# A hybrid decoder layer on one core: three steps of window attention instead of four and a half after each chunk of the input projection's last block

## The chip, the core and the metric

The kernel runs on one core of a Trainium2 chip. The metric is the device time of one execution in microseconds (us), the median of several runs. TensorE is called PE in the profile (PEld is its weight loads), VectorE is DVE, ScalarE is ACT, GpSimd is POOL, and SP issues the DMAs of this kernel.

## What is computed

One decoder layer over 2048 tokens of width 1024, in float32. Cut to what matters here:

```python
proj = rms_norm(x) @ w_in                     # 2176 columns = 17 chunks of 128
qa, ka, va, pb, qm = split_cols(proj, ...)
out_a = sliding_window_attention(qa, ka, va)  # 6 heads, blocks of 128 queries, 256 keys in the band
out_b = rwkv7_mixer(pb)                       # a recurrence over the tokens, 6 heads
out_m = memory_attention(qm, mk, mv)          # 4 heads, 256 memory tokens
x = x + concat(out_a, out_b, out_m) @ w_out
x = x + conv_ffn(rms_norm(x))                 # silu(gate) * val, then w_down
```

## The kernel before, in words

The tokens are cut into 4 blocks of 512 for the large products and into 16 tiles of 128 for attention and the recurrence (RWKV). Every large product takes three matmuls for one (each operand is split into a high and a low part: `whi`, `wlo`, `hh`, `hl`), so a chunk of the projection or of the output product is 24 matmuls of 128x512 (`proj`, which writes the PSUM tile `mm`).

**Input projection** (`ip`): for each block, 17 chunks in the order of `ORDER`; `g` counts the chunks from 0 to 67, so the last block is g = 51 to 67. After each chunk `post` reads the result out of PSUM. The last five chunks of each block (0, 1, 2, 15, 16) are the queries of the window and memory attention; they are split in `qhi` and `qlo`, stored to DRAM (`dq`), and the last of them starts a power on POOL that gives the queries' norms (`rsb`). In the last block all chunks go to one PSUM buffer, `mm`; in the others two take turns:

```python
o = self.proj(ps, w.pop(g), hh, hl, "mm" if g % 2 or b == NB - 1 else "po")
```

**Attention** (`attention`) is a generator with six steps for each of the 16 tiles of queries: window of the first kv head, window of the second, memory logits, values (two steps), and the rest of the memory attention. Tile i reads the queries of its own tokens, so tiles 12 to 15 need the last block of the projection, with its `dq` and `rsb`; tiles 0 to 11 do not. On PE it is `pl`, `tpa`, `po`, `plm`, `tpm` and `pm`; on DVE mostly `lg` and `em`.

**RWKV** (`rwkv`) is a second generator, four steps for a tile: front (`pz`, `pc`), `pg` and `tpb`, a triangular inverse of 31 times two small DVE operations (`xtmp`, `xinv`) between two trips through DRAM (`nbd` to `nb`, `xbd` to `xa`), and the chain over two half tiles (`pq`, `pu`, `pS`).

**Output product** (`outproj`): for each block of 512 it loads the concatenated results (`cr`), splits them (`ch`, `cl`) and runs 8 chunks with the weights `w_op`. Its pool of SBUF takes the place of the projection's pools, so it can begin to load only when the last chunk's `post` has let go of them. Block 0 of it needs tiles 0 to 3 of attention and RWKV, block 1 tiles 4 to 7, and so on. The feed-forward part follows.

**What sets the order.** All of this is recorded first, and a list scheduler (`Recorder.order`) then puts the instructions of each engine in order by dependencies and priorities. The order of recording counts in two ways: it decides who gets which buffer of a ring after whom (`slots`; the PSUM rings `ip` and `po` are shared by `post` and attention), and with that the length of the paths from which the priorities come. `side(g)` is called after chunk g and decides how many steps of RWKV and attention are recorded there; what is left of both is recorded after the projection, one step of each in turn, in `run`. Every instruction is issued through one helper, so all rows of the profile carry line 349, and the names of the tiles tell them apart.

Of the kernel before, what the change touches and what calls it, by code (L numbers as in the profile page):

```python
# [129 lines left out]
class Recorder:  # L130
# [93 lines left out]
    def margin(self, d, o):  # L224

        return 0 if d.eng == o.eng or None in (d.eng, o.eng) else MARGIN

# [33 lines left out]
    def run(self):  # L261
# [35 lines left out]
        while True:  # L297
# [17 lines left out]
            if soon[e] and o.dur > 150:  # L315
                c = min((c for c in soon[e] if c[0] < t + min(WAIT, o.dur) and c[2].level > o.level), default=None)
                if c:
# [41 lines left out]


WAIT = 100
MARGIN = 300
SLACK = 1500
WR = 4
# [49 lines left out]
class K:  # L414
# [1064 lines left out]
    def run(self):  # L1479
# [64 lines left out]
        atn = []  # L1544

        def side(g):
            for _ in range(starts.get(g, 0)):
                next(rw, None)
            if atn and (g - 52) * 72 // 16 >= 0:
                for _ in range((g - 51) * 72 // 16 - (g - 52) * 72 // 16):  # L1550
                    next(atn[0], None)
        for n, b in (("t", 2), ("w", 4), ("h", 1), ("x", 4)):
            p[n] = pool(n, b, side="right")
# [2 lines left out]
        def x_done():  # L1556
# [3 lines left out]
            p["a"] = pool("a", 2)  # L1560
            atn.append(self.attention(p, ps))
        self.ip(p, ps, side, x_done)
        for n in ("h", "w", "t"):
            rec.close(p[n])
# [130 lines left out]
```

## Time and profile before

| | |
|---|---|
| median of 3 runs | 2493.63 us (2492.27 to 2495.86) |
| profiled execution, its own time | 2499.48 us |
| its span, first to last instruction | 2497.6 us |
| mean granted TensorE clock | 0.968 of full speed |
| busy: PE, DVE, ACT, POOL | 95%, 81%, 49%, 8% of the span |

The span is what the rows further down lie in; the profiled execution's own time is 1.9 us longer, and 5.85 us above the median. Busy PE time is not PE at its peak, since matmuls overlap and are slower when the clock is lowered. Times in rows are us from the span's start.

### The profile page before, as it was taken

What the parts mean: (1) busy time and instruction counts of PE and PEld (TensorE: products, weight loads), DVE (VectorE), ACT (ScalarE), POOL (GpSimd) and SP (SyncE); (2) the same over time, 40 slices, a digit from 0 to 9 for tenths busy, and PEclk for the clock granted to TensorE, in tenths of its full rate; (3) what the DMA queues carried; (4) which work ended last, traced back from release to release, by engine and by line L of the source; (5) the groups of instructions that cost most, each with busy time, mean ns of one, the idle gap of its engine ahead of it and who ended that gap; (6) DMA issues with size and microseconds to landing.
All of it is one profiled execution on the core that took longest, in us unless ns stands there. A gap on an engine that the chain in (4) does not pass through costs nothing.

```text
span 2497.6 us, 36689 instructions
## 1 busy us (share of the span) xinstructions
PE 2372.4 (95%) x12268; PEld 1886.0 (76%) x12268; DVE 2015.2 (81%) x4614; ACT 1219.6 (49%) x2413; POOL 190.2 (8%) x292
## 2 busy tenths in 40 slices
PE   8899989899899979999899999999999998999999
PEld 6677777676666757777788888888888876888887
DVE  7579677878878777759588998899888887888876
ACT  6354544555445544555355455565555463444442
POOL 1112212211111121100000000000000000000000
PEclk9999999899989989999999999999999998999999
DMA  7586746744434465557233733354323246558443
GB/s 226 176 246 179 214 127 176 190 131 137 138 106 132 118 192 157 168 162 238 81 117 110 261 119 117 115 179 137 106 93 113 100 150 214 162 155 275 148 141 129
DMA packets 292933, 389.30 MB, mean 156 GB/s; under 512 B 49911, under 2 KB 155392, under 8 KB 292744
## 3 DMA queue, kind: packets, MB, share of 16 engines
q1 hardware_dynamic: 292744, 386.96, 49.8%
q8 instruction: 97, 1.59, 0.3%
q14 instruction: 92, 0.75, 0.1%
HBM read 274.89 MB, written 111.97 MB: 155 GB/s over the span
## 4 chain that ended last, share of the span: by engine, by line
PE 80%; DVE 8%; DMA 7%; issue 3%; ACT 1%; SPq 0%; POOL 0%; POOLq 0%; DVEq 0%; ACTq 0%
PE uf L349 28%; PE mm L349 16%; PE uch L349 14%; PE uip L349 7%; PE pq L349 4%; PE po L349 2%; PE pg L349 1%; DMA nb<-nbd 1%; PE tpa L349 1%; DVE xtmp L349 1%; DVE wlo L349 1%; PE pl L349 1%; PE st L349 1%; DVE xinv L349 1%; DMA wraw<-w_down_in 1%
## 5 line engine op out<-in xcount | busy, mean ns | idle before, releaser
L349 ACT CAST whi<-wraw 128x512 fp32r<-128x512 f32 (+1 forms) x410 | 250.2, 613 | 423.7 <-PE uf L349 148.9
L349 PE MATMUL uf<-h2h,wlo 128*128 128x512 f32 x1056 | 412.2, 392 | 15.3 <-DVE wlo L349 15.3
L349 PE MATMUL uf<-h2h,whi 128*128 128x512 f32 x1056 | 412.7, 392 | 4.7 <-ACT whi L349 4.6
L349 PE MATMUL uf<-h2l,whi 128*128 128x512 f32 x1056 | 412.6, 391 | 0.0
L349 DVE TENSOR_TENSOR wlo<-wraw,whi 128x512 fp32r<-128x512 f32 (+1 forms) x410 | 276.2, 677 | 89.1 <-ACT whi L349 87.7
L349 ACT CAST whi<-ws 128x512 fp32r<-128x512 f32 (+1 forms) x272 | 164.6, 609 | 288.5 <-PE uf L349 151.1
L349 DVE SCALAR_TENSOR_TENSOR uc<-ub,pp,uc 128x1024 f32<-128x1024 f32 x176 | 224.2, 1278 | 26.0 <-ACT uc L349 26.0
L349 PEld LDWEIGHTS uf<-h2h,wlo 128*128 128x128 f32 x1056 | 199.5, 189 | 59.0 <-DVE wlo L349 17.5
L349 PE MATMUL mm<-hh,whi 128*128 128x512 f32 x544 | 228.0, 420 | 15.6 <-DVE sh L349 5.4
L349 PEld LDWEIGHTS uf<-h2h,whi 128*128 128x128 f32 x1056 | 199.3, 189 | 48.4 <-ACT whi L349 6.4
L349 PEld LDWEIGHTS uf<-h2l,whi 128*128 128x128 f32 x1056 | 199.5, 189 | 41.8 <-DVE h2l L349 0.4
L349 PE MATMUL mm<-hl,whi 128*128 128x512 f32 x544 | 223.3, 411 | 2.0 <-DVE hl L349 1.9
L349 PE MATMUL mm<-hh,wlo 128*128 128x512 f32 x544 | 222.9, 410 | 0.0
L349 PE MATMUL uch<-h2h,whi 128*128 128x512 f32 x528 | 205.6, 389 | 0.0
L349 PE MATMUL uch<-h2h,wlo 128*128 128x512 f32 x528 | 205.5, 390 | 0.0
L349 PE MATMUL uch<-h2l,whi 128*128 128x512 f32 x528 | 205.4, 389 | 0.0
L349 DVE TENSOR_TENSOR wlo<-ws,whi 128x512 fp32r<-128x512 f32 (+1 forms) x272 | 178.5, 667 | 10.6 <-ACT whi L349 10.1
L349 PEld LDWEIGHTS mm<-hh,whi 128*128 128x128 f32 x544 | 106.6, 196 | 46.8 <-DVE sh L349 6.0
L349 ACT CAST h2h<-tr 128x512 fp32r<-128x512 f32 x182 | 110.0, 619 | 60.3 <-DMA tr<-dg 44.8
L349 ACT ACTIVATE uc<-ub,pp 128x1024 f32<-128x1024 f32 x88 | 109.4, 1244 | 38.4 <-DVE ub L349 37.1
L349 PEld LDWEIGHTS mm<-hl,whi 128*128 128x128 f32 x544 | 106.6, 196 | 25.8 <-DVE hl L349 3.4
L349 DVE TENSOR_TENSOR h2l<-tr,h2h 128x512 fp32r<-128x512 f32 x182 | 119.9, 684 | 7.3 <-ACT h2h L349 7.2
(363 smaller groups left out, 4702.8 us busy)
## 6 DMA issues: line engine op xcount, KB each, us to landing
wraw<-w_up_in SPq DMA_DIRECT2D x176, 256.0 KB
tr<-dg SPq DMA_DIRECT2D x154, 256.0 KB
wraw<-w_ip_in SPq DMA_DIRECT2D x136, 256.0 KB
dg<-uc SPq DMA_DIRECT2D x88, 256.0 KB
dg<-tt SPq DMA_DIRECT2D x66, 256.0 KB
wraw<-w_op_in SPq DMA_DIRECT2D x64, 256.0 KB
wraw<-w_down_in SPq DMA_DIRECT2D x64, 256.0 KB
xk<-xT_in SPq DMA_DIRECT2D x56, 256.0 KB
```

The costliest lines, as they stand in the source:

```text
L349: getattr(getattr(nc, o.eng), o.fn)(*map(real, o.a), **{k: real(v) for k, v in o.k.items()})
```

## The change

It changes how many attention steps `side` records after each of the 16 chunks g = 52 to 67: 72 steps over 16 chunks (4 or 5 after each, 12 tiles of attention in all) become 48 (3 after each, 8 tiles). The other 48 of the 96 steps, 24 more than before, are recorded after the projection with the rest of RWKV.

```diff
+EARLY = 48
...
-            if atn and (g - 52) * 72 // 16 >= 0:
-                for _ in range((g - 51) * 72 // 16 - (g - 52) * 72 // 16):
+            if atn and g >= 52:
+                for _ in range((g - 51) * EARLY // 16 - (g - 52) * EARLY // 16):
                     next(atn[0], None)
```

No instruction is added or removed: PE has 10764 matmuls, DVE 4614, ACT 2235 and SP 1594 instructions in both programs. On PE the first 667 and the last 6111 stand in the same order; the 3986 between them do not, because the priorities change. Counted in the order: the first matmul of the projection's last block with a recorded attention step (g = 52) is number 2071 before and 2250 now, its last number 3826 before and 3522 now, and the first of the output product number 3908 before and 3693 now.

The last matmuls on PE ahead of the output product's first, `mm<-ch`, in the program before. `pl` is the window logits of attention tile 12, the others belong to tile 11 and, `pz`, to RWKV:

```order
L349 MATMUL tpb<-cst,bk 128x128 x6
L349 MATMUL plm<-km,dq 128x256 x4
L349 MATMUL po<-pt,va 64x384 x2
L349 MATMUL pz<-w_488,lw 128x384
L349 MATMUL tpm_10276<-cst,em 128x128 x4
L349 MATMUL st<-cst,sq 128x128 x4
L349 MATMUL pm<-ptm,vm 64x128 x4
L349 MATMUL tpm_10329<-cst,em 128x128 x4
L349 MATMUL pm<-ptm,vm 64x128 x4
L349 MATMUL pl<-ka,dq 128x256 x10
L349 MATMUL mm<-ch,whi 128x512
```

The same place now; `tpa`, `po` and `plm` are of attention tile 8, and `pq`, `pc`, `pu` and `pS` are the RWKV chain and front:

```order
L349 MATMUL pS<-uv,bkt 64x64 x6
L349 MATMUL tpa<-cst,lg 128x128
L349 MATMUL pq<-uv,gmk 64x64 x5
L349 MATMUL po<-pt,va 64x384
L349 MATMUL pq<-S_112,ar 128x128 x3
L349 MATMUL tpa<-cst,lg 128x128 x5
L349 MATMUL pc<-cst,sg 128x130 x3
L349 MATMUL pu<-qa,X_124 64x64 x6
L349 MATMUL plm<-km,dq 128x256 x4
L349 MATMUL mm<-ch,whi 128x512
```

Between the last projection matmul and the first output matmul there stood 81 matmuls, and 170 stand there now, with more of attention (18 `tpa` instead of 12, 12 `plm` instead of 4) and of the RWKV chain (30 `pq` instead of 6, 18 `pu` instead of none). Attention tile 12, which needs the projection's last chunk, has moved behind. The 24 matmuls of the first output chunk are spread over 79 places instead of 30. Between the last matmul of one projection chunk and the first of the next, for the 15 boundaries from g = 52 to 67, stood 31 other matmuls on average and 10 at least; now it is 27 and 7.

The SP queue at the same place, before. `dq<-dq` is the load of attention tile 12's queries, `dq__1446<-qlo` the store of the last chunk's queries, `cr` the first loads of the output product:

```order
L349 DMA dq__1446<-qhi 64x4x128 x2
L349 DMA rr<-drk__714 128x1536
L349 DMA nbd_10243<-gmk 32x12x32 x2
L349 DMA dq__1446<-qlo 64x4x128 x2
L349 DMA va<-dv__1313 128x128
L349 DMA dcat__3560<-cat 128x384
L349 DMA dq<-dq__1446 128x2x640
L349 DMA cr<-dcat__3560 128x4x128 x3
L349 DMA nb<-nbd_10243 96x1x1024
L349 DMA xbd_10388<-xinv 96x256
L349 DMA wraw<-w_op_in 128x512
```

And now, where `dq<-dq` is the load of tile 8's queries:

```order
L349 DMA dq<-dq__1446 128x2x640
L349 DMA va<-dv__1313 128x128
L349 DMA nbd_9415<-gmk 32x12x32 x2
L349 DMA dq__1446<-qlo 64x4x128
L349 DMA dcat__3126<-cat 128x384
L349 DMA xa<-xbd_9171 32x6x32
L349 DMA uv<-dv__1313 64x384
L349 DMA cr<-dcat__3126 128x4x128 x2
L349 DMA nb<-nbd_9415 96x1x1024
L349 DMA dcat__3126<-cat 128x256
L349 DMA cr<-dcat__3126 128x4x128
L349 DMA wraw<-w_op_in 128x512
```

The load of the queries that the next attention tile reads has moved ahead of the last store `dq__1446<-qlo`, and the first loads of the output product keep their place behind that store.

## Rows read from the trace of the kernel before

**Rows 1.** Busy time by stage: stretch, its length, busy of each engine, PEclk, DMA.

```profile
146.00:464.00 318.00, 303.00 (x1818) 241.58 (x1817) 253.32 (x739) 153.63 (x321) 62.75 (x79) 0.98 0.61 181
464.00:864.00 400.00, 364.91 (x2515) 263.92 (x2515) 317.05 (x1224) 206.25 (x600) 69.34 (x125) 0.92 0.48 134
864.00:892.00 28.00, 17.65 (x119) 12.13 (x119) 23.69 (x105) 13.41 (x35) 8.64 (x3) 0.81 0.69 185
892.00:920.00 28.00, 22.72 (x98) 15.62 (x98) 22.08 (x81) 13.99 (x40) 3.97 (x12) 0.76 0.75 207
920.00:1061.00 141.00, 137.47 (x936) 102.88 (x936) 101.80 (x348) 69.51 (x178) 20.70 (x42) 0.98 0.54 161
```

**Rows 2.** The timeline around the projection's end: start, length, engine, operation, [idle before].

```profile
863.69 0.39 PE L349 MATMUL mm<-hh,wlo 128*128 128x512 f32 x1
...
873.83 1.25 SPq L349 DMA_DIRECT2D dq__1446<-qlo  x2
...
877.36 1.56 SPq L349 DMA_DIRECT2D cr<-dcat__3560  x3
...
879.50 6.85 POOL L349 TENSOR_TENSOR rsb<-rsb,mh 128x40 f32<-128x40 f32 x1 [1.72 <-DVE rsb L349]
...
882.63 0.62 ACT L349 CAST ch<-cr 128x512 fp32r<-128x512 f32 x1 [1.83 <-DMA cr<-dcat__3560]
...
886.39 0.88 DVE L349 SCALAR_TENSOR_TENSOR lg<-pl,rsb,bias 128x256 f32<-128x256 f32 x2 [0.74 <-POOL rsb L349]
...
889.60 0.19 DVE L349 TENSOR_TENSOR xtmp<-xinv,nb 96x31 f32<-96x31 f32 x1 [1.36 <-DMA nb<-nbd]
...
891.62 0.80 PE L349 MATMUL mm<-ch,whi 128*128 128x512 f32 x1 [2.53 <-ACT whi L349]
```

**Rows 3.** What PE waited for from 864 to 924: total, times, longest.

```profile
PE pl L349 <- DVE lg L349: 3.9, 1, 3.9
PE mm L349 <- ACT ch L349: 2.7, 1, 2.7
PE mm L349 <- ACT whi L349: 2.5, 1, 2.5
```

**Rows 4.** PE busy and clock in slices of 10 us.

```profile
870.00:880.00 10.00, 7.73 (x59) 1.00 0.67 184
880.00:890.00 10.00, 3.54 (x17) 0.57 0.95 250
910.00:920.00 10.00, 9.17 (x52) 0.66 0.29 100
```

**Rows 5.** PE's timeline: two neighbours at the lower clock, two at the full one.

```profile
681.68 0.63 PE L349 MATMUL mm<-hl,whi 128*128 128x512 f32 x1
682.11 0.63 PE L349 MATMUL mm<-hh,wlo 128*128 128x512 f32 x1
...
684.57 0.39 PE L349 MATMUL mm<-hl,whi 128*128 128x512 f32 x1
684.79 0.39 PE L349 MATMUL mm<-hh,wlo 128*128 128x512 f32 x1
```

**Rows 6.** Groups of PE instructions, 100 to 1210 us: busy, mean ns.

```profile
L349 PE MATMUL po<-pt,va 128*64 128x384 f32 x124 | 51.5, 528 | 1.7 <-DMA nbd<-gmk 0.9 <-ACT pt L349 0.7
L349 PE MATMUL tpa<-cst,lg 128*128 128x128 f32 x186 | 37.9, 308 | 6.4 <-DVE lg L349 5.7 <-ACT em L349 0.4
L349 PE MATMUL pl<-ka,dq 128*128 128x256 f32 x180 | 41.6, 324 | 9.6 <-DVE lg L349 8.0 <-DVE xtmp L349 1.5
L349 PE MATMUL pm<-ptm,vm 128*64 128x128 f32 x256 | 27.5, 292 | 1.9 <-ACT ptm L349 1.4 <-ACT cat L349 0.6
L349 PE MATMUL plm<-km,dq 128*128 128x256 f32 x128 | 25.4, 314 | 2.9 <-DVE lg L349 1.9 <-ACT pt L349 1.0
L349 PE MATMUL tpm<-cst,em 128*128 128x128 f32 x128 | 22.3, 290 | 2.8 <-DVE em L349 2.1 <-DVE xtmp L349 0.7
```

**Rows 7.** Reading a chunk out of PSUM, 464 to 864 us: groups of ACT and DVE.

```profile
L349 ACT ACTIVATE raw<-mm,om 128x512 f32<-128x512 f32 x10 | 6.8, 683 | 6.0 <-PE mm L349 6.0
L349 DVE SCALAR_TENSOR_TENSOR sh<-mm,pp,raw 128x511 f32<-128x511 f32 x6 | 4.5, 742 | 0.4 <-ACT carry L349 0.4
```

**Rows 8.** PE's waits from 480 to 800 us: the chunks of the projection on PSUM's readers.

```profile
PE mm L349 <- DVE sh L349: 4.1, 1, 4.1
```

## The prediction

> **What bounds the kernel now.** I read the page first, then the busy time by stage, then the timeline and PE's waits at the one stage that stands out, and last the order of the two programs. The page says that PE is the engine that sets the time (95% busy, 80% of the chain that ended last). The order says where the change can act: the first 667 and the last 6111 matmuls keep their places. In the trace that frozen part ends at about 146 us and begins again at about 1061 us, and every instruction is still there once. So only the 915 us between can change, and only through two things: how long PE idles there and at what clock it runs.
>
> The stages [rows 1] tell where that is. In the projection's last block (464 to 864 us) PE idles 400 - 364.9 = 35.1 us, 8.8%, at a mean clock of 0.92. From 864 to 892 it idles 10.3 of 28 us at 0.81, from 892 to 920 5.3 of 28 us at 0.76. After that, to 1061, 3.5 of 141 us (2.5%) at 0.98. The 56 us from 864 to 920 hold 15.6 of the 69.3 us of idle time in the whole stretch.
>
> Why there: twelve tiles of attention are recorded before the projection ends, and these are all that can run without its last block. The timeline [rows 2] shows all three sources of PE work dry at once. The last projection matmul is at 863.7; its queries are stored at 873.8, and only then come the output product's loads (877.4), their split (882.6) and its first matmul (891.6). Attention tile 12 waits for the queries' norms, 6.85 us on POOL from 879.5, so that its first `lg` is at 886.4. RWKV's next inverse waits for `nb` until 889.6. PE's longest waits [rows 3] are these: `pl` on `lg` 3.9 us, `mm` on `ch` 2.7 and on `whi` 2.5. The clock follows [rows 4]: 1.00 in the slice from 870, 0.57 in the next, in which PE was busy 3.5 of 10 us, and still 0.66 from 910, where PE was busy again.
>
> **The change part by part.** It costs nothing in instructions; four tiles of attention (8 to 11) are recorded after the projection instead of inside its last block. A tile is about 206/16 = 12.9 us of busy PE (the six groups of [rows 6] add to 206), so some 52 us of PE work move. The order also moves RWKV: 179 matmuls more now stand before chunk 52 (PE number 2250 instead of 2071), some two tiles of RWKV, and one tile more stands behind the projection.
>
> *The gap at the end of the projection.* Before, 81 matmuls stood in it, and PE was busy 17.65 us in those 28 us [rows 1], 0.218 us each. Now 170 stand there, so about 37 us of PE work, more than the 28 us that the stores, loads and splits take. Tile 8's queries and norms come from an earlier block, so it waits for neither `dq` nor `rsb`. I let this stretch keep the last block's own share of idling, 8.8%: 37 x 0.088 = 3.3 instead of 10.3, a gain of 7.0 us. From 892 to 920 the first output chunk now has 55 other matmuls among its 24 (it spans 79 places, before 30), so its waits for `ch` and `whi` are covered too: 28 x 0.088 = 2.5 instead of 5.3, a gain of 2.8. Then the clock. At the lower level, 1.2 GHz, a matmul takes 0.43 us, at 2.4 GHz 0.22 to 0.23 [rows 5], so a shortfall of the mean clock costs about its own share of the busy time. The stage lost 0.19 x 17.65 + 0.24 x 22.7 = 8.8 us; at the last block's 0.92 it would lose 0.08 x 51 = 4.1, a gain of 4.7. Together **-14.5 us**. The bounds are 0 (the new work waits as the old did) and -24.4 (15.6 + 8.8, no idling and full clock).
>
> *The stages around it.* The last block loses 304 matmuls (3826 - 3522, at 364.9/1756 = 0.208 us each 63 us busy, 69 us long): its idling falls by 69 x 0.088 = 6.1 us and its clock loss by 0.08 x 63 = 5.0. The stage before it gains 179 matmuls, 37 us, at its own rates (15 of 318 us idle, 0.98): +1.8 and +0.8. The stage after 920 grows from 141 to about 185 us (63 us moved behind, 19 of them in the gap) and has more attention and less dense work in it. Before, it idled 2.5%; the last block, with more attention, 8.8%. With the mean of the two, and of the clocks (0.95), it idles 10.5 us instead of 3.5 (+7.0) and loses 9.3 us of clock instead of 2.8 (+6.5). Sum -6.1 - 5.0 + 2.6 + 13.5 = **+5.0 us**. If it keeps its old rates, that is 4.6 and 3.7 us instead of 3.5 and 2.8, and the sum -6.5. If it takes the last block's rates (16.3 and 14.8), it is +16.3. I take the middle, since per us its new mix lies between the two stages.
>
> *The chunk boundaries.* All chunks of the last block use one PSUM buffer, so between two of them PE needs other work until ACT and DVE have read the first: 0.68 + 0.74 = 1.43 us [rows 7] when neither queues. Fewer attention steps could lay this bare. In the order they do not: between the chunks of g = 52 to 67 stand 31 other matmuls on average before and 27 now, at least 10 before and 7 now, and at 0.208 us seven are 1.46 us. The trace shows one real wait of this kind, 4.1 us [rows 8]. I price it at 0, since RWKV fills the places that attention left; with the cover gone at every one of the 15 boundaries it is 15 x 1.43 = 21.5 us. The Trainium skill speaks against the change here: "Perfetto Trace Analysis", section "Matmuls", says that independent matmul groups should rotate through different PSUM banks, so that the readout of one overlaps the next group. By that rule the boundaries bind when cover is taken out, and the sum would be -9.5 + 21.5 = +12; the one wait in the trace agrees that the dependency is there, and the order says it stays covered.
>
> The sum: -14.5 + 5.0 = **-9.5 us**, so 2499.5 - 9.5 = 2490 us on the profiled execution's own footing. That execution is 5.85 us above the median of the runs shown, so for the median I say **2484 us**.
>
> **The rivals.**
> *The tail takes over the waits.* The gap closes, but the stage after it runs at the last block's rates: -14.5 + 16.3 = +1.8, 2495 us. For it: PE's waits inside attention are on DVE (`lg`, `em`) [rows 6] and move with the tiles. Against it: after 920 the stage already holds most of tiles 13 to 15 and idles 2.5% [rows 1]. It decides when that stage idles over 7% at a clock under 0.93. Chance 0.22.
> *Boundaries laid bare,* the slower one, by the mechanism just priced: 2499.5 + 12 - 5.85, 2506 us. It decides once more than 10 of the 15 boundaries wait their 1.43 us (9.5 + 5 us lost). Smaller prices of the same place, and an early stage that doesn't absorb its two tiles of RWKV, end between 2499 and 2506. Chance of slower 0.20.
> *The gap closes wholly* and the tail keeps its rates: -24.4 - 6.5 = -31, 2463 us. For it: the three waits of [rows 3] all have work in front of them now. Against it: that work is small matmuls that wait for ACT and DVE themselves. Chance that the gain is over 17 us: 0.13.
> *It does nothing:* the scheduler could have put the instructions as before whatever was recorded; the order excludes this.
>
> **How the numbers follow.** The forecast, a gain of 5 to 17 us, has 0.45. With the large gain, faster by over 0.2% has 0.58; the first rival gives within 0.2% (5 us, about what a measurement of this kernel can tell from no change) 0.22; slower has 0.20. The bounds of the two terms together are -31 and +16. The range from 2467 to 2501 leaves out the last part on each side, some 0.07 below and 0.13 above. The forecast's own range is 2477 to 2489.
>
> **What would show it.** The last projection matmul should be near 830 us (864 + 40 for the stage ahead, less 63 + 6 + 5); the first output matmul 30 to 45 us later; between them PE over 90% busy and no slice of 10 us with a clock near 0.57; `lg` of tile 12 should no longer wait for `rsb` with PE idle. The stage after it, up to the last matmul whose place is unchanged, should idle 4 to 7% and end near 1051 us, 10 earlier than now. From there on the two traces should run alike, with the same 1437 us to the end (2498 - 1061). Wrong would be: an end of that stage later than 1061 us with PE waiting on DVE for `lg` (the first rival) or `mm` waiting on `sh`, `raw` or `qlo` at most boundaries (the second); or a longer first part, before the last block, which I let run at its old rates.

## The result and the profile after

| | before | now |
|---|---|---|
| median, runs taken in turn on one chip | 2494.74 us (2492.27 to 2498.06) | 2469.17 us (2466.69 to 2471.70) |
| profiled execution, its own time | 2499.48 us | 2466.69 us |
| its span | 2497.6 us | 2464.8 us |
| mean granted TensorE clock | 0.968 | 0.977 |

The ratio is 0.9895 with a 95% interval of 0.9881 to 0.991: the changed kernel is 25.6 us faster, well past the 0.2% that can be told from no change. The forecast was 2484, a gain of 9.5. The two profiled executions differ by 32.8 us, because that of before lies 4.7 us above its median and that of now 2.5 us below; stages are compared on this larger footing. Each stage below is read from one execution, and that can lie up to 13 us off its kernel's median (with 36 and with 60 steps, further down, it lies 12.7 and 11.5 us above).

The busy time of the changed kernel by stage answers to [rows 1]: up to the last block, the last block, the gap up to the output product's first matmul, the 28 us after it, the stage after that, and the unchanged rest. Columns: stretch, length, busy PE, PEld, DVE, ACT and POOL (with instructions), PEclk, DMA share, GB/s.

```profile
146.00:495.00 349.00, 330.37 (x2090) 258.96 (x2088) 282.15 (x885) 166.43 (x360) 76.61 (x109) 0.99 0.60 177
495.00:777.00 282.00, 266.11 (x1791) 197.55 (x1790) 232.44 (x897) 148.44 (x424) 43.45 (x81) 0.95 0.50 144
777.00:818.40 41.40, 37.84 (x278) 28.20 (x277) 30.48 (x105) 25.03 (x71) 12.72 (x16) 0.75 0.72 201
818.40:847.00 28.60, 23.83 (x139) 15.85 (x138) 25.00 (x101) 14.38 (x41) 3.06 (x2) 0.88 0.54 155
847.00:1027.50 180.50, 172.04 (x1161) 125.15 (x1159) 138.37 (x503) 97.07 (x273) 24.45 (x54) 0.99 0.52 155
1027.50:2464.80 1437.30, 1400.46 (x6200) 1147.50 (x6199) 1205.26 (x1930) 695.43 (x1115) 5.54 (x5) 0.99 0.45 149
```

What a stage loses is told here as its idle PE time plus its length times what the clock lacks to 1 (a clock printed with two digits leaves a few us open over the 900 us). It isn't time itself: it charges the clock for idle time too, and it takes the busy time at the full clock as given. In these terms, and with before cut at the same events:

| stage | before: length, loss | now: length, loss | loss, change | forecast |
|---|---|---|---|---|
| up to the last block | 318.5, 21.4 | 348.9, 22.1 | +0.7 | +2.6 |
| last block | 399.2, 67.0 (35.1 idle) | 282.0, 30.0 (15.9 idle) | -37.0 | -11.1 |
| gap and 28 us after | 55.9, 27.6 (15.6 idle) | 69.5, 21.8 (8.3 idle) | -5.8 | -14.5 |
| after that, to the unchanged part | 140.6, 6.3 | 181.0, 10.3 | +4.0 | +13.5 |

The rest takes 1437 us in both. The four changes add to -38.1, while the stretch became 32.8 us shorter. So the gain was found elsewhere than looked for: the last block gave 37 us of loss, the gap two fifths of what was forecast.

The timeline around the projection's end, for [rows 2]: start, length, engine, operation, [idle before].

```profile
776.87 0.48 PE L349 MATMUL mm<-hh,wlo 128*128 128x512 f32 x1
...
791.66 1.88 SPq L349 DMA_DIRECT2D cr<-dcat__3126  x2
791.78 6.75 POOL L349 TENSOR_TENSOR rsb<-rsb,mh 128x40 f32<-128x40 f32 x1 [2.81 <-DVE rsb L349]
791.83 0.88 DVE L349 SCALAR_TENSOR_TENSOR lg<-pl,rsb,bias 128x256 f32<-128x256 f32 x2
...
795.16 0.62 ACT L349 CAST ch<-cr 128x512 fp32r<-128x512 f32 x1 [2.30 <-DMA cr<-dcat__3126]
...
808.88 0.62 ACT L349 CAST whi<-wraw 128x512 fp32r<-128x512 f32 x1
...
818.37 0.39 PE L349 MATMUL mm<-ch,whi 128*128 128x512 f32 x1
```

The last projection matmul is at 777 (before 864, forecast 830) and the first output matmul 41.5 us later (forecast 30 to 45). Its operand `ch` is split at 795, and the first of its weights `whi` is ready at 809.5, so the last 9 us until 818 are its place behind other work, not a wait for data. `lg` of a tile of an earlier block runs at 791.8, the moment POOL begins its power for the last one's `rsb`: the waits of [rows 3] are covered. PE's waits from 777 to 830, the answer to [rows 3] (total, times, longest):

```profile
PE px L349 <- ACT TD L349: 2.0, 1, 2.0
PE tpa L349 <- ACT em L349: 1.0, 1, 1.0
```

And PE busy and PEclk in slices of 10 us there, for [rows 4]:

```profile
780.00:790.00 10.00, 10.00 (x88) 1.00 0.69 196
790.00:800.00 10.00, 7.47 (x59) 0.80 0.70 200
800.00:810.00 10.00, 8.97 (x63) 0.50 1.06 264
810.00:820.00 10.00, 10.00 (x58) 0.68 0.57 179
```

In the slice from 790 PE idled 2.5 us and the clock fell to its lower level, 1.2 GHz, and it stayed there while PE was busy 90 to 100%.

Within the last block the losses are lumped. Before, in three stretches of 25 us (columns as in the first view), the first at the block's start:

```profile
464.00:489.00 25.00, 16.64 (x57) 12.70 (x57) 21.12 (x90) 11.04 (x30) 9.09 (x3) 0.73 0.89 213
...
664.00:689.00 25.00, 16.97 (x72) 12.07 (x72) 21.02 (x84) 6.31 (x15) 1.97 (x2) 0.80 0.59 178
689.00:714.00 25.00, 21.77 (x123) 13.99 (x123) 17.86 (x70) 11.94 (x40) 3.96 (x13) 0.66 0.29 81
```

These 75 us hold 19.6 us of idling and 6.8 + 5.0 + 8.5 = 20.3 of clock, 39.9 of the block's 67.0; the other 324 us lose 8.4%. What stands behind the longest wait for a chunk's readout, in DVE's timeline of before:

```profile
674.58 0.68 DVE L349 TENSOR_TENSOR sh<-sh,lnb 128x512 f32<-128x512 f32 x1
676.34 0.19 DVE L349 TENSOR_TENSOR xtmp<-xinv,nb 96x31 f32<-96x31 f32 x1 [1.08 <-DMA nb<-nbd]
676.45 0.74 DVE L349 SCALAR_TENSOR_TENSOR sh<-mm,pp,raw 128x511 f32<-128x511 f32 x1
```

`sh<-mm`, which frees the PSUM buffer for the next chunk, stands on DVE behind other work (until 675.3) and behind an `xtmp` of the RWKV inverse that waits 1.1 us for its `nb` from DRAM. PE gets its chunk at 677.25, after the 4.1 us of [rows 8]. After that the inverse's short dependent operations and attention's `lg` take turns on DVE, and PE waits for `lg` three more times, 3.3 us in all. At the block's start it is other waits, for the readout `kp` 2.7 us, for `lg` 3.1, for the weights `whi` 2.1 and for `hl` 1.2. The same places now:

```profile
495.00:520.00 25.00, 21.59 (x143) 17.13 (x141) 24.75 (x106) 15.58 (x41) 9.04 (x5) 1.00 0.85 224
635.00:655.00 20.00, 16.49 (x98) 11.93 (x97) 16.92 (x61) 6.32 (x19) 3.10 (x12) 0.83 0.55 155
655.00:675.00 20.00, 18.19 (x149) 13.28 (x147) 16.74 (x51) 11.55 (x37) 1.05 (x2) 0.87 0.47 137
675.00:695.00 20.00, 20.00 (x97) 13.17 (x97) 6.78 (x24) 6.16 (x18) 4.41 (x13) 0.71 0.30 93
```

The block's start keeps its clock (143 matmuls in 25 us instead of 57) and loses 3.4 us instead of 15.1; the place in its middle loses 17.1 instead of 24.8; the other 197 us lose 9.5, 4.8%. So what is left is lumped too (17.1 of 30.0 us in 60 us), and of the 37 us the start gave 11.7, the middle 7.7 and the rest 17.6, most of that by being 127 us shorter.

One kind of wait runs through the whole block. PE's waits there that involve attention's `lg` on DVE, with the readout `kp`, before:

```profile
PE pl L349 <- DVE lg L349: 6.4, 5, 2.5
PE tpa L349 <- DVE lg L349: 5.7, 3, 3.0
PE mm L349 <- DVE kp L349: 2.7, 1, 2.7
```

and those for `lg` now:

```profile
PE pl L349 <- DVE lg L349: 1.2, 1, 1.2
PE tpa L349 <- DVE lg L349: 0.9, 2, 0.7
```

With `plm` (0.4 us) PE waited ten times and 12.5 us for `lg` before, and three times and 2.1 us now. That is over half of the 19.2 us by which its idling in the block fell, and more than in proportion: by the recorded order the block holds 7.3 tiles of attention instead of 11.3.

### The profile page after: what moved, and what is told of

It reads as the page before. It is cut to its first block, busy times and chain, and to the rows that moved or that the text cites. A ratio compares the mean times of both kernels' runs of the same rounds, so it can differ in the third digit from the quotient of the medians.

```text
span 2464.8 us, 36670 instructions
## 1 busy us (share of the span) xinstructions
PE 2357.6 (96%) x12268; PEld 1876.5 (76%) x12268; DVE 2008.0 (81%) x4614; ACT 1216.6 (49%) x2413; POOL 185.1 (8%) x292
## 4 chain that ended last, share of the span: by engine, by line
PE 77%; DVE 10%; DMA 7%; issue 4%; ACT 1%; SPq 1%; POOL 0%; POOLq 0%; DVEq 0%; ACTq 0%
PE uf L349 27%; PE mm L349 15%; PE uch L349 13%; PE uip L349 7%; PE pq L349 4%; PE pg L349 2%; PE po L349 2%; DMA nb<-nbd 2%; DVE wlo L349 1%; DVE uc L349 1%; DVE lg L349 1%; PE tpa L349 1%; SPq L349 1%; DVE xtmp L349 1%; DVE xinv L349 1%
## 5 line engine op out<-in xcount | busy, mean ns | idle before, releaser
L349 PEld LDWEIGHTS uf<-h2h,wlo 128*128 128x128 f32 x1056 | 199.2, 189 | 59.3 <-DVE wlo L349 17.8
L349 PE MATMUL mm<-hh,whi 128*128 128x512 f32 x544 | 225.4, 416 | 19.2 <-DVE sh L349 6.3
L349 DVE TENSOR_TENSOR wlo<-ws,whi 128x512 fp32r<-128x512 f32 (+1 forms) x272 | 178.6, 668 | 10.6 <-ACT whi L349 10.2
```

Source lines behind the costliest of these rows:

```text
L349: getattr(getattr(nc, o.eng), o.fn)(*map(real, o.a), **{k: real(v) for k, v in o.k.items()})
```

## The experiments

The theory after the result: (A) the last block's gain comes from its being thinner in attention, whatever the order otherwise. The rivals: (B) it is the luck of the one order that the list scheduler made of the new recording; (C) the gain is the filled gap after all, and the block only shifted its losses. The forecasts made ahead of the runs use other letters: their theory A, or gap theory, is (C) here, their B, or pace theory, is (A), and their C, or accident theory, is (B). All kernels are compared with before on the same chip; edits are against the changed kernel unless said. Only the number and the places of the attention steps and the scheduler's numbers differ; every kernel does the whole work. Where the scheduler's numbers differ, the order outside the stretch changes too, and its end is cut at 1437.4 us ahead of the kernel's end, as in the others.

### How many steps

```diff
-EARLY = 48
+EARLY = 66
```

The others have 36, 60, 54 and 70 in its place.

> EARLY = 66, one tile of attention (six steps) behind the projection instead of four. By the order, 175 matmuls stand in the gap between the projection and the output product (81 before, 170 with 48), but the last block still holds 9.5 tiles of attention and 6.5 of RWKV (11.3 and 7.5 before; 7.3 and 4.5 with 48). Theory A, the covered gap is what was gained: 15 to 25 us faster than before, as with 48. Theory B, the thinner last block is what was gained, in proportion to the tiles taken out of it (3 of 7): about 8 to 12 us faster, and the block idles 7 to 8%. Theory C, the gain is an accident of one schedule: anything from 10 us slower to 25 us faster, without relation to either count.

> EARLY = 36, six tiles of attention behind the projection; by the order only 55 matmuls stand in the gap (fewer than the 81 before), and the last block holds 5.6 tiles of attention and 5 of RWKV. Theory A: the gap is open again, so most of the gain is lost, 0 to 8 us faster than before. Theory B: the block is as thin as with 48, so 20 to 28 us faster than before, less what the stage behind it gives back with two more tiles (0 to 10 us). Theory C: no relation.

> EARLY = 60, 3 or 4 steps after each chunk, between 66 and 48. By the order 8.8 tiles of attention and 6 of RWKV stand in the last block and 173 matmuls in the gap. Loss below means PE's idle time plus the clock's shortfall (one minus the mean granted clock, times the length). Pace theory (the block loses 17% of its length with 4.5 steps per chunk and 10 to 11% with 4.1 or fewer): 25 to 32 us faster than before, with a loss in the block of 10 to 12%. Accident theory (each order has its own loss, without relation to the pace): the block's loss anywhere from 10 to 18%, 10 to 32 us faster. Gap theory: as with 66, about 30 us faster, with the difference in the gap.

> EARLY = 54, 3 or 4 steps after each chunk; by the order 8.2 tiles of attention and 5 of RWKV in the last block, 117 matmuls in the gap. Pace theory: 24 to 32 us faster than before, the block's loss 10 to 12%. Accident theory: the block's loss anywhere from 10 to 18%. Gap theory: half of the gain of 66, some 12 to 18 us, since the gap holds only 36 matmuls more than before instead of 94.

> EARLY = 70: only two steps, the values of tile 11, are recorded behind the projection; 10.3 tiles of attention and 7 of RWKV in the block, 161 matmuls in the gap. If what counts is that the last step of tile 11 no longer has to be done before the projection ends: 20 to 30 us faster than before, like 66. If the gain grows with the steps taken out (6 steps gave 31 us): about 8 to 12 us.

| steps | median us (before on that chip) | ratio, 95% | block: length, loss | gap and 28 us after, loss | tail: length, loss |
|---|---|---|---|---|---|
| 36 | 2488.83 (2494.33) | 0.999 (0.9963 to 1.0016) | 285.5, 17.2% | 17.8 | 239.2, 30.2 |
| 48 | 2469.17 (2494.74) | 0.9895 (0.9881 to 0.991) | 282.0, 10.6% | 21.8 | 181.0, 10.3 |
| 54 | 2471.20 (2497.09) | 0.9891 (0.9877 to 0.9906) | 293.6, 8.6% | 14.8 | 173.5, 9.5 |
| 60 | 2462.70 (2497.09) | 0.9861 (0.9827 to 0.9896) | 321.7, 11.7% | 26.3 | 163.3, 10.2 |
| 66 | 2463.31 (2494.33) | 0.9875 (0.9859 to 0.9892) | 333.2, 10.6% | 21.6 | 150.5, 6.4 |
| 70 | 2477.74 (2495.83) | 0.9929 (0.9905 to 0.9953) | 352.5, 10.6% | 16.1 | 143.5, 5.6 |
| 72, before | 2494.74 | 1 | 399.2, 16.8% | 27.6 | 140.6, 6.3 |

Already 66 steps bring all of the gain and 70 two thirds of it, although hardly any attention is moved behind the projection (the tails are 150 and 144 us long). So it isn't the amount moved that pays. Nor does the gap order them: the traced run with 60 steps loses 26.3 us there, nearly as much as before, and at 2474.15 us it is still 25 us shorter than the one of before. PE's waits for `lg` in the block are 1.9 us with 36 steps, 2.1 with 48, then 5.3, 5.5, 4.8 and, with 70, 1.8; with 72 they are 12.5. Of the forecasts, that for 54 steps came out in its time (25.9 us). 60 and 66 gained more than any number given (34.4 and 31.0), 70 (18.1) lies between its two, and 36 (5.5) is where the gap theory had it, but its gap loses only 17.8 us. The last block of 66 steps, by the busy time of its stretch:

```profile
466.80:800.00 333.20, 314.70 (x2233) 229.00 (x2234) 278.44 (x1075) 181.09 (x524) 60.84 (x108) 0.95 0.50 146
```

It idles 18.5 us at 0.95, where 72 steps idled 35.1 at 0.92. With 36 steps the other end shows, in the last block and the tail:

```profile
488.60:774.10 285.50, 270.66 (x1659) 199.06 (x1659) 213.14 (x799) 130.52 (x362) 39.99 (x69) 0.88 0.47 137
...
823.20:1062.40 239.20, 223.36 (x1528) 160.88 (x1527) 182.07 (x692) 127.43 (x369) 32.42 (x71) 0.94 0.48 148
```

The tail idles 15.8 us (6.6%) at 0.94: that is the first rival of the prediction, at nearly the point that it named, but for a step more than this change makes. The block is no more idle than with 48 steps (14.8 us), and yet it loses 34 us of clock. Not all of this need belong to 36 steps: the traced run took 2501.5 us, among ten from 2480.7 to 2504.7, with a mean clock of 0.963 over the whole span, where the six from 2480.7 to 2489.5 had 0.968 to 0.973.

### Which chunks are thinned

```diff
-                for _ in range((g - 51) * EARLY // 16 - (g - 52) * EARLY // 16):
+                upto = lambda k: min(EARLY, k * 72 // 16)
+                for _ in range(upto(g - 51) - upto(g - 52)):
```

This keeps the old pace of four and a half steps until 48 are recorded and then stops. A second kernel starts late and then keeps the old pace to the end:

```diff
-                for _ in range((g - 51) * EARLY // 16 - (g - 52) * EARLY // 16):
+                upto = lambda k: max(0, k * 72 // 16 - 24)
+                for _ in range(upto(g - 51) - upto(g - 52)):
```

> 48 steps as in the changed kernel, but at the old pace of 4 or 5 after each of the first 11 chunks and none after the last five. The same tiles (8 to 15) are left for the stages behind the projection; by the order 110 matmuls stand in the gap. Theory A: 18 to 26 us faster than before, since the same tiles wait behind the projection. Theory B, if it is the pace of attention between the chunks that makes PE wait: only 5 to 15 us faster, with the first two thirds of the last block idling 8 to 9% as before and the rest less. Theory C: no relation.

> 48 steps at the old pace of 4 or 5, but after the last 11 chunks instead of the first 11 (none after the first five). Pace theory: as the version with the first 11 chunks, 10 to 18 us faster than before, with the chunks without attention at a small loss and the rest at 17%. If instead the start of the block is what loses (in the trace before, PE idles 8.5 us from 464 to 490 where attention begins), about 20 to 28 us faster. Accident theory: no relation.

The first gave 2479.32 us (ratio 0.9943, 0.9927 to 0.9959), 15.0 us under before and so where the pace theory had it; the second 2466.23 (0.9874, 0.9831 to 0.9917), 30.9 us under before, more than either forecast. The last block of the first:

```profile
480.00:813.30 333.30, 300.64 (x2081) 222.97 (x2082) 258.33 (x982) 165.15 (x468) 58.28 (x104) 0.92 0.48 139
```

At the old pace the block loses 59.3 us, 17.8%, as before, and PE waits 8.7 us in it for `lg`. The gap and the 28 us after it lose 12.6 us instead of 27.6, a gain of 15.0 where 14.5 was forecast for it; the tail loses 10.2 instead of 6.3, and the stage ahead of the block 29.8 instead of 21.4. So the gain of a filled gap is real and of the size forecast, and it shows apart from the thinner block. In the changed kernel itself it is smaller, 5.8, and rival C falls there. With the late start the block loses 13.2% (6.7 us for `lg`), the gap and what follows 11.9 us, and the tail 17.7.

### The order with the number of steps kept

The list scheduler has numbers of its own. Other ones give other orders of the same recording, so pairs with 72 and 48 steps under the same numbers tell (A) from (B). In the kernels with 72 steps the old line or `EARLY = 72` stands, which records the same.

```diff
-MARGIN = 300
+MARGIN = 320
...
-SLACK = 1500
+SLACK = 1300
...
-WAIT = 100
+WAIT = 140
```

Each number was changed alone; two more pairs have MARGIN 360 and SLACK 1800.

> The kernel before with one number of the scheduler changed that has nothing to do with attention: MARGIN, the time it adds between engines, 320 instead of 300 ns. The order changes in many places, the counts of tiles by stage hardly (11.3 and 7.5 tiles in the last block, 75 matmuls in the gap). Theories A and B: within 5 us of the kernel before. Theory C, that any other order of this stage moves the time by as much as the change did: 10 us or more away, either way.

> The changed kernel with the scheduler's MARGIN at 320 instead of 300 ns, which reorders much but keeps the pace of three steps (7.3 tiles of attention and 4.5 of RWKV in the block, 125 matmuls in the gap). Pace theory: 20 to 30 us faster than before, the block's loss 10 to 12%, as in the changed kernel. Accident theory: off by 10 us or more from the changed kernel, most likely toward the kernel before, with a loss in the block of 14% or more.

> 72 steps with MARGIN 360 instead of 300 ns. Nothing is recorded elsewhere, but the scheduler itself leaves more behind the projection: 10.4 tiles of attention and 7 of RWKV in the block, 191 matmuls in the gap instead of 81. Gap theory: 10 to 20 us faster than before, with the loss in the gap and the 28 us behind it down from 28 to some 15 us and the block's loss unchanged near 17%. If the gain of the versions with 66 and fewer steps comes from what is recorded where, and not from what stands in the gap: within 8 us of the kernel before.

> 48 steps with MARGIN 360, the pair of the 72 steps in the same setting, which took 2486.0 us. If the number of steps is worth some 20 to 25 us in any order: 2458 to 2468 us. If the change only met a better order: 2475 to 2495 us.

> The kernel before (72 steps) in another order: the scheduler's SLACK for transfers 1300 instead of 1500 ns. 11.1 tiles of attention and 7.5 of RWKV in the last block, 99 matmuls in the gap. If 72 steps are slow in themselves: within 8 us of the kernel before, with a loss (idle time plus the clock's shortfall) of 16 to 18% in the last block. If the order before was an unlucky one among equals: 10 us or more faster.

> 48 steps with SLACK 1300, the pair of the 72 steps in the same setting, which took 2467.6 us. If the number of steps is worth some 20 to 25 us in any order: 2440 to 2450 us. If the change only met a better order: 2460 to 2475 us, no faster than its pair.

> 72 steps with the scheduler's WAIT 140 instead of 100 ns; the same places of the stages as in the kernel before (11.2 tiles of attention and 7.5 of RWKV in the block, 71 matmuls in the gap), but 1868 lines of difference on PE. If 72 steps are slow in themselves: 2485 to 2500 us. If order is luck: anywhere from 2465 to 2500 us.

> 48 steps with WAIT 140, the pair of the run before. If the number of steps is worth some 20 to 25 us in any order: 15 to 30 us faster than its pair, with a loss in the last block of 10 to 12% where its pair has 16 to 18%. If order is luck: no faster than its pair.

> 72 steps as before, but the scheduler's SLACK is 1800 instead of 1500, which gives another order: 181 matmuls instead of 81 stand in the gap, the block still begins at matmul 2071. If 72 steps cost the last block in any order, the block loses 15 to 18.5% of its length, and the time is above that of the same numbers with 48 steps by 10 to 30 us. If the gain was the luck of one order, the pair shows under 5 us or the other sign.

> 48 steps under SLACK 1800. First theory: the block loses 7 to 14%, and the time is 10 to 30 us under that of 72 steps with the same SLACK, some 2465 us. Rival, luck of the order: within 5 us of it or above.

| numbers | 72 steps: us, ratio to before, block's loss, waits for `lg` in it | 48 steps: the same | difference of ratios |
|---|---|---|---|
| as they were | 2494.74, 1, 16.8%, 12.5 us | 2469.17, 0.9895, 10.6%, 2.1 us | -1.05% |
| MARGIN 320 | 2492.20, 0.9996, 17.5%, 11.5 us | 2455.46, 0.9827, 7.2%, 0.8 us | -1.69% |
| MARGIN 360 | 2486.02, 0.9958, 17.3%, 10.2 us | 2460.11, 0.9855, 13.8%, 1.8 us | -1.03% |
| SLACK 1300 | 2467.63, 0.9884, 15.5%, 7.3 us | 2468.53, 0.9882, 8.5%, 1.5 us | -0.02% |
| SLACK 1800 | 2497.09, 0.9997, 16.6%, 12.3 us | 2476.67, 0.9931, 9.9%, 3.5 us | -0.66% |
| WAIT 140 | 2534.90, 1.0154, 18.5%, 14.0 us | 2524.98, 1.0112, 16.1%, 3.5 us | -0.42% |

The 95% intervals of these ratios reach 0.0012 to 0.0028 to each side; the two of a pair ran on different chips under MARGIN 320, MARGIN 360 and SLACK 1300, so the ratios are compared. The mean difference is -0.81%, some 20 us; the single ones go from nothing to 42 us. In all six pairs the block loses a larger share with 72 steps, 15.5 to 18.5%, and with 48 mostly 7 to 14%. In all six PE also waits longer for `lg` there, in ten to fourteen waits with 72 steps and in two to five with 48. So these two go with the number of steps under every order tried.

The time follows them only loosely. With SLACK 1300 the block's loss falls from 59.5 to 24.0 us and that of the whole stretch by 24.1, and yet the stretch is just 3.1 us shorter (882.5 instead of 885.6): PE is busy for longer at the full clock instead, and why was not located. In the other five pairs the stretch is 15 to 43 us shorter. Of the forecasts, the pairs under MARGIN 360 and SLACK 1800 came out as the theory of the thinner block had them with 48 steps; under SLACK 1300 luck of the order did; under MARGIN 320 the gain was larger and under WAIT 140 smaller (9.9 us) than forecast. Two last blocks under MARGIN 320, first with 72 steps:

```profile
468.50:865.60 397.10, 363.51 (x2514) 263.23 (x2514) 315.31 (x1223) 205.63 (x600) 61.94 (x125) 0.91 0.47 134
```

and with 48:

```profile
492.70:764.60 271.90, 257.80 (x1799) 192.00 (x1797) 234.80 (x917) 147.89 (x422) 45.63 (x80) 0.98 0.54 155
```

The first has a lump like that of before (PE busy 4.25 us from 670 to 680, 7.02 and 6.40 in the next two slices), and PE's waits in its block are of the same kinds:

```profile
PE tpa L349 <- DVE lg L349: 8.0, 5, 3.6
PE mm L349 <- DVE sh L349: 3.9, 1, 3.9
```

The second, at 2455.46 us (0.9806 to 0.9848), is the fastest of all, 42 us under before on its chip (2497.09). WAIT 140 shows how much the order alone can cost: 37 us with 72 steps, outside both of its forecasts. PE's longest waits of that kernel from 146 to 1100 us:

```profile
PE pl L349 <- DVE lg L349: 11.4, 9, 4.5
PE mm L349 <- ACT whi L349: 8.2, 2, 7.9
PE pl L349 <- DMA xa<-xbd: 6.4, 1, 6.4
```

SLACK 1300 with 72 steps gains 28 us with the block at 15.5%. Its stretch from 146 us to the rest loses 106.5 us, before 124.1, now 86.6; that explains 18 of the 28. By length, 11.2 us of the gain lie ahead of the block and 16.0 in it.

Two kernels with 72 steps also test the filled gap. By the recorded order 191 matmuls stand in it with MARGIN 360 and 181 with SLACK 1800, as many as with 48 steps (170). The gap and the 28 us after it with MARGIN 360 (columns: stretch, length, busy PE, PEclk, DMA share, GB/s):

```profile
828.30:877.50 49.20, 43.25 (x299) 0.83 0.47 130
877.50:905.50 28.00, 18.27 (x55) 0.70 0.87 229
```

PE idles 15.7 us there (before 15.6), and the loss is 32.4 us where some 15 were forecast; with SLACK 1800 it idles 16.3 and loses 29.8, with one wait of 7.8 us for the output product's `whi`. So the number of matmuls in the gap doesn't close it; what each waits for does count.

A last one asked whether a better order rescues 36 steps:

```diff
-EARLY = 48
-MARGIN = 300
+EARLY = 36
+MARGIN = 260
```

> 36 steps with MARGIN 260 instead of 300 ns: 5.3 tiles of attention and 4 of RWKV in the block, 62 matmuls in the gap. If 36 is too few in itself, since then too much is left behind the projection: within 10 us of the kernel before, with a loss of 25 us or more in the stage behind the gap. If the first order with 36 was an unlucky one: 15 us or more faster than before.

It gave 2481.48 us (0.9937, 0.9917 to 0.9958), 14.4 us under before and between its two forecasts. Its block loses 11.1%, so the 17.2% is not the price of 36 steps in itself but came with that order or that run; its tail (248 us) still loses 29.3 us, so in both orders with 36 steps the tail costs some 30 us.

So neither (A) nor (B) stands alone. Under the same numbers fewer steps gain some 20 us on the average, with the last block's loss and PE's waits for `lg` lower in every pair, though in one pair that gained no time; the particular order is worth as much again, to either side.

## Why the prediction was wrong

**What bounds the kernel** was right: only the stretch from 146 us to the unchanged part changed, and that part took the same 1437 us. But idling and the clock are not the only two things that can change in it: under SLACK 1300 a stretch with 24 us less of both was just 3 us shorter. The end of the stretch came at 1027 instead of the 1051 that was forecast. Against the sum of -9.5 the terms were off by -25.9 (last block), +8.7 (gap), -9.5 (tail) and -1.9 (stage ahead).

**The step that failed is the one on the last block**, "The last block loses 304 matmuls (3826 - 3522 ...): its idling falls by 69 x 0.088 = 6.1 us and its clock loss by 0.08 x 63 = 5.0." It was priced at -11.1 and measured -37.0. Two things are wrong in it.

The count: 304 is how far the block's *last* matmul moved in the order. Its first one moved too, by the 179 that the stage ahead took over, so the block went from 1756 to 1273 places and lost 304 + 179 = 483. At the prediction's own rates that is 100 us busy, 110 us long, 9.7 us of idling and 8.0 of clock, -17.7. With it the sum would have been -16.1 instead of -9.5. The same slip put the end of the projection at 830, which also subtracts 5 us of clock that the 0.208 us of a matmul already hold; 864 + 40 - 110 is 794, and it came at 777. The stage ahead grew by 30 us and not by 40, and the block shrank by 117.

The rates: the prediction let the block keep 8.8% idling and 0.92 for what remained of it. The other 19 us of the 37 are that it did not: its loss fell from 16.8% to 10.6%. It went by a mean over 400 us, of which 40 of the 67 us of loss lay in 75 us, and let the waits shrink with the length. They shrank by more: PE's waits for `lg` fell from 12.5 to 2.1 us, and over half of the block's fall in idling is theirs. The pairs show both under all six orders: 15.5 to 18.5% of loss and 7.3 to 14.0 us for `lg` with 72 steps, 0.8 to 3.5 us for `lg` with 48. The kernel with the old pace on its first chunks keeps them (17.8%, 8.7 us), and the one with 70 steps has lost them (10.6%, 1.8 us). Why just two steps fewer are enough isn't settled: the orders differ in many places, and which of them decides was not tried.

**The gap** was forecast right in its idling and wrong in its clock. It idled 3.6 of 41.5 us (forecast 3.3 of 40), PE was busy 91%, its longest waits of before are covered, and the first output matmul came when forecast. But the 28 us behind idled 4.8 (forecast 2.5), and the clock of the gap was 0.75 instead of 0.92, a loss of 10.4 us there. "No slice of 10 us with a clock near 0.57" was wrong: one was at 0.50. The forecast's clock term has a slip of its own: it takes 0.08 x 51, two stretches of 28 us, where its 37 us in the gap and 25.5 behind it make 62.5, so 5.0 instead of 4.1. With the 48 steps placed otherwise the forecast was met: gap and 28 us after lose 12.6 us in the kernel with the old pace first, 11.9 in the one with the late start, against a forecast of 27.6 - 14.5 = 13.1. With 72 steps and as many matmuls in the gap, under two other orders, it was not (32.4 and 29.8). The term's mechanism holds where the work in the gap doesn't wait itself.

**The stage ahead** took its 179 matmuls for +0.7 us (forecast +2.6). **The tail** is 181 us long, near the 185 forecast, and loses 10.3 us instead of 19.8: it kept nearly its old rates (4.7% idling, clock 0.99). Its new mix costs little with 48 steps or more at an even pace, under the scheduler's own numbers, and 30 us with 36; under other numbers 48 steps cost 11 to 21 us there.

**The chunk boundaries** were rightly priced near 0: the waits did not grow. PE's waits in the last block now, the longest first:

```profile
PE mm L349 <- DVE sh L349: 3.4, 2, 2.5
PE po L349 <- ACT pt L349: 3.0, 2, 1.7
PE mm L349 <- DVE ks L349: 1.5, 3, 0.7
```

`sh` and `ks`, the readouts, cost 4.9 us over all boundaries; before, `sh` and `kp` cost 4.1 and 2.7. The rival's price of 21.5 us was not paid: RWKV and attention still cover the single buffer. The Trainium skill ("Perfetto Trace Analysis", section "Matmuls") says that independent groups of matmuls should rotate through PSUM banks. The trace has 4.9 us of the waits that this would spare; no run here gives the block a second buffer.

**The rivals.** "The gap closes wholly" came near in size, 2463 us, by the wrong cause: the gap gave 6 of the profiled 33 us. "The tail takes over" came nearly true with 36 steps (6.6% idle at 0.94). "Boundaries laid bare" came true nowhere. No rival allowed for the last block's rates changing, nor for an order that is better or worse by itself; of the 18 kernels with other steps or numbers, the times lie between 2455 and 2535 us. The range, 2467 to 2501, held the time by 2 us, and that is luck: the end of the range that it fell on stood for a gap that closes.

## What to carry to other kernels

Where the losses of a long stage are lumped, cut it into slices and list what the engine waits for before pricing a share of it: here a mean rate times the length removed missed that one kind of wait nearly went. When a list scheduler remakes the order, count both ends of every stage in the new order, and take the result as one draw: run the same change under two or three other settings of the scheduler before crediting the edit. A filled gap is worth its idle time only where the work put into it doesn't wait itself, and its clock only if no drought is left in it.

## What was not expected of the hardware

The clock stays at its lower level while the trace shows PE busy. In the changed kernel, in slices of 2 us (busy PE, PEclk):

```profile
794.00:796.00 2.00, 0.17 (x2) 0.99 0.85 245
796.00:798.00 2.00, 1.80 (x8) 0.50 0.50 151
...
814.00:816.00 2.00, 2.00 (x5) 0.50 0.82 259
816.00:818.00 2.00, 2.00 (x24) 0.89 0.29 111
```

PE idled for 2.0 us from 794.2, the clock was at 0.50 from 796 on, and it came back at 816 only, with PE busy for 18.8 of those 20 us. With 36 steps two shorter pauses, of 0.40 and 0.73 us, stand ahead of 16 us at 0.50, with PE busy for all of them:

```profile
574.00:576.00 2.00, 1.60 (x21) 1.00 0.23 69
576.00:578.00 2.00, 1.27 (x9) 1.00 0.41 131
...
580.00:582.00 2.00, 2.00 (x5) 0.50 1.00 338
...
594.00:596.00 2.00, 2.00 (x9) 0.50 0.33 106
596.00:598.00 2.00, 2.00 (x11) 0.90 0.03 8
```

What ran there, from 580 to 596 us, was a mix of `pg`, `po`, `tpa`, `tpm` and `pl` with few projection matmuls. So a PE that the trace shows busy was no sign of the higher clock here; what decides it was not tried. The Trainium skill ("TensorE: Matmul & The Clock Gate", Part 1) puts the penalty of the clock's ramp, the warm-up at a kernel's start, at under 1% of a typical span. The drops above come in the middle of the kernel, so that figure isn't about them; the mean granted clock was 0.968 before and 0.977 now.
